# Changing the order of the high and low matmuls in a few groups of a one-core diffusion backbone

## The chip, the core and the metric

The kernel runs on one core of a Trainium2 chip. The metric is the device time of one execution in microseconds. Three executions of the kernel before were timed, and one more was run under the hardware profiler; the trace of that one is what all rows below come from.

## The reference, cut to what matters

The model has two layers over 256 latent tokens of width 2048, with a context prefix of 256 tokens. What bears on the change is the large projections: tall fp32 products of 256 tokens with weight matrices that are each used once.

```
# layer 0 (retention and Fourier mixing, gated)
yx = concat(retention(q, k, v) * silu(ga), fourier(u) * silu(gb)) @ w_out      # 4096 -> 2048
x  = x + gate_x * yx
# layer 1 (short gated convolution)
bg, cg, xt, g = split(h @ w_in, 4)                                             # 2048 -> 4 x 4096
y  = bg * conv3(cg * xt) * silu(g)
x  = x + gate_x * (y @ w_out)                                                  # 4096 -> 2048
return rmsnorm(x, final_norm_w)
```

## The kernel before

All activations are kept transposed, channels on partitions and 256 tokens along the free dimension. To keep fp32 accuracy with TensorE's fp32r format, every operand is split into a high part and a low part that is the rest. An activation tile holds both beside each other, high in columns 0 to 255 and low in columns 256 to 511. A weight tile of 1 MB (`raw`, 128 partitions by 2048) comes by DMA and is cut in four quarters of 512 columns: ScalarE casts a quarter into `whi` (line 94), VectorE subtracts and writes `wlo` (line 59). Each of the two has six buffers.

`group_t` (line 131) computes 256 output channels for 256 tokens into one PSUM tile `gT` with two halves of 128 channels, m = 0 and 1. It goes over `nkt` weight tiles (4 in the two output projections, 2 elsewhere), each with four quarters. A quarter holds four 128 by 128 blocks, j = 0 to 3, for two slices of input channels and the two halves m = j mod 2. Each block takes two matmuls: the **high** one, H, with the block of `whi` against all 512 columns of the activation (high and low part), and the **low** one, L, with the block of `wlo` against the 256 high columns. A pair H and L is so 768 columns. In the rows a high matmul reads `gT<-...,whi` with 128x512, and a low one `gT<-...,wlo` with 128x256. Each matmul has its own weight load (`LDWEIGHTS`, engine PEld).

The order of the eight matmuls of a quarter is one of three lists, written out by hand:

```
LOW = "L0 H0 L1 H1 L2 H2 L3 H3".split()
HIGH = "H0 L0 H1 L1 H2 L2 H3 L3".split()
MIRRORED = "H0 L0 L1 H1 H2 L2 L3 H3".split()
```

`LOW` is the rule. With `settle` set, the first weight tile of the group has its quarters in the order LOW, MIRRORED, MIRRORED, HIGH, and the rest of the group is LOW again. This is set in nine groups: in `project` (line 816), which runs for the output projection of layer 0 (`w0o`) and of layer 1 (`w1o`), for output blocks 1 and 3 of 8; and in the loop of layer 1 over 16 channel blocks (line 874), where each block has four groups in a row (`tcg`, `txt`, `tbg`, `tg`), in `tcg` of blocks 1, 2 and 8 and in `tbg` of blocks 0 and 1. The last block of each projection uses `group_d` (line 156) instead, in which all matmuls are 256 columns wide, and the value projections of layer 0 use `group_n`, in which all are 512 wide.

A scheduler orders the instructions of an engine from the order of the code and an estimate of when operands are ready. Around the output projection of layer 0 it mixes groups with the Fourier work (`pz`, `pP`, `py`), and around block 0 of layer 1 it mixes two groups. From block 1 of layer 1 to the end of block 6 of `w1o` the groups stand one behind another on TensorE.

Of the kernel before, what the change touches and what calls it, by code (L numbers as in the profile page):

```python
# [35 lines left out]
def body(tc, a, out):  # L36
    nc = tc.nc
    es = ExitStack()
    with es:
# [6 lines left out]
        def psum(name):  # L46
            return pp.tile([P, 2, 512], F32, tag="ps", name=name)

        def bank(name):
            return ap.tile([P, 512], F32, tag="bk", name=name)  # L50

        def act_tile(tag, name):
            return acts.tile([P, 2, 512], F32R, tag=tag, name=name)

        def mm(o, l, r, start, stop):
            nc.tensor.matmul(o, l, r, start=start, stop=stop, skip_group_check=True)  # L56
# [4 lines left out]
        def mul(o, x, y):  # L61
            nc.vector.tensor_tensor(o, x, y, op=ALU.mult)

        def add(o, x, y):
            nc.vector.tensor_tensor(o, x, y, op=ALU.add)  # L65
# [17 lines left out]
        def load_raw(src):  # L83
            raw = wp.tile([P, 2048], F32, tag="raw", name="raw")
            nc.sync.dma_start(raw[:], src)
            return raw
# [10 lines left out]
        def split_w(raw, spare=None):  # L97

            parts = []
            for pc in range(4):  # L100
                w = tuple(t[:] for t in spare()) if spare and pc == 3 else slot()
                cut(raw[:, pc * 512:(pc + 1) * 512], *w)
                parts.append(w)
            return parts
# [7 lines left out]
        def bg():  # L112

            if quiet[0]:
                return
            turn[0] ^= 1
            if tasks and (turn[0] or often[0]):
                tasks.pop(0)()

        def hook():  # L120
            if stages:
                f = stages.pop(0)
                if f is not None:
                    f()


        LOW = "L0 H0 L1 H1 L2 H2 L3 H3".split()
        HIGH = "H0 L0 H1 L1 H2 L2 H3 L3".split()
        MIRRORED = "H0 L0 L1 H1 H2 L2 L3 H3".split()

        def group_t(wd, i0, nkt, streams, settle=False):

            ps = [psum("gT") for _ in streams]
            last = nkt * 8 - 1
            for kt in range(nkt):
                raw = load_raw(wd[i0 + kt])
                bg()
                for pc, (hi, lo) in enumerate(split_w(raw)):
                    todo = LOW
                    if settle and kt == 0 and pc:  # L140
                        todo = HIGH if pc == 3 else MIRRORED
                    seen = set()
                    for what, j in ((x[0], int(x[1])) for x in todo):
                        k2, m = j // 2, j % 2
                        kc, c0 = kt * 8 + pc * 2 + k2, j * 128
                        n = 512 if what == "H" else 256
                        w = (hi if what == "H" else lo)[:, c0:c0 + 128]
                        for t, st in zip(ps, streams):
                            mm(t[:, m, 0:n], w, st[kc // 2][:, kc % 2, 0:n], kc == 0 and j not in seen,
                               kc == last and j in seen)  # L150
                        seen.add(j)
                    if pc % 2:
                        hook()
            return ps
# [40 lines left out]
        def lr(pool, t, name="t2", bufs=5, ring=5):  # L195

            r = pool.tile([P, 2, 256], F32, tag="t2", bufs=ring, name="lr_r")
            nc.scalar.copy(r[:], t[:, :, 256:512])  # L198
            s = pool.tile([P, 2, 256], F32, tag=name, bufs=bufs, name=name)
            add(s[:], t[:, :, 0:256], r[:])  # L200
            return s

        def rstd_bc(pool, ps_sum, n):

            r = pool.tile([P, 256], F32, tag="rstd", bufs=2, name="rstd")
            nc.scalar.activation(r[:], ps_sum, AF.Sqrt, bias=eps[:], scale=1.0 / n)
            nc.vector.reciprocal(r[:], r[:])
            return r
# [277 lines left out]
        for pr in range(4):  # L486
# [23 lines left out]
            def heads():  # L510
                return [retention(hh, mk[hh], q, k, kc, lambda: vbox[0]) for hh in range(2)]

            if pr == 0:
# [4 lines left out]
                h0, h1 = heads()  # L518
                stages += [None, h0[0], h1[0], h0[1], h0[2], h1[1], None, h1[2]]
                keep((pvx, pvc))  # L520
            elif pr < 3:
                k, kc = keys()
                q = queries()
                h0, h1 = heads()
# [3 lines left out]
            else:  # L528
# [6 lines left out]
                h0, h1 = heads()  # L535
# [8 lines left out]
            for hh, hd in enumerate((h0, h1)):  # L544
                y = yA[2 * pr + hh] = act_tile(YA[2 * pr + hh], f"yA{2 * pr + hh}")
                t = hd[3]["t"]
# [269 lines left out]
        def project(wd, xs, gcol, xin, acc, first=None, post=None):  # L816


            def res(b, m, v, src):
                nc.vector.scalar_tensor_tensor(x1[b][:, m, :], v, mods[:, gcol + 2 * b + m:gcol + 2 * b + m + 1],  # L820
                                               src[:, m, :], op0=ALU.mult, op1=ALU.add)

            tot = None
            for b in range(8):
                src = xin(b)
                quiet[0] = b >= 7 - (post is not None)
                if b < 7:
                    t = first if b == 0 and first is not None else group_t(wd, 4 * b, 4, [xs], b in (1, 3))[0]
                    s = lr(l1, t)
                    for m in range(2):  # L830
                        res(b, m, s[:, m, :], src)
                    if b == 0:
                        nc.scalar.square(acc[:], x1[b][:])
                    else:
                        sq = l1.tile([P, 2, 256], F32, tag="t2", bufs=5, name="sq")
                        nc.scalar.square(sq[:], x1[b][:])
                        add(acc[:], acc[:], sq[:])
                    for m in range(2 if post is not None else 0):
                        nc.scalar.activation(x1[b][:, m, :], x1[b][:, m, :], AF.Copy,
                                             scale=cols[:, post + 2 * b + m:post + 2 * b + m + 1])  # L840
                else:
                    t = group_d(wd, 4 * b, 4, xs)
                    tot = bank("tot")
                    for m in range(2):
                        mm(tot[:, 0:256], ones[:], acc[:, m, :], m == 0, False)

                    warm = l1.tile([P, 1], F32, tag="warm", name="warm")
                    nc.scalar.activation(warm[:], acc[:, 0, 0:1], AF.Sqrt)
                    sq = l1.tile([P, 2, 256], F32, tag="t2", bufs=5, name="sq")
                    for m in range(2):  # L850
                        res(b, m, t[:, m * 256:m * 256 + 256], src)
                        nc.scalar.square(sq[:, m, :], x1[b][:, m, :])
                        mm(tot[:, 0:256], ones[:], sq[:, m, :], False, m == 1)
            return rstd_bc(l1, tot[:, 0:256], D)
# [13 lines left out]
        h1 = [act_tile(HF[e], f"h1_{e}") for e in range(8)]  # L868
# [3 lines left out]
        w1 = a["w1"]  # L872
        y1 = []
        for b in range(16):
            settle = b in (1, 2, 8)
            tcg, = group_t(w1, b * 8, 2, [h1], settle)
            scg = lr(l1, tcg, "scg", 2)
            txt, = group_t(w1, b * 8 + 2, 2, [h1])
            z = lr(l1, txt, "z", 2)
            mul(z[:], z[:], scg[:])  # L880
            cv = l1.tile([P, 2, 256], F32, tag="cv", bufs=2, name="cv")
            for m in range(2):
                w = [cols[:, C_CV + j * 32 + 2 * b + m:C_CV + j * 32 + 2 * b + m + 1] for j in range(3)]
                z4 = z[:, m, :].rearrange("p (r w) -> p r w", w=64)
                c4 = cv[:, m, :].rearrange("p (r w) -> p r w", w=64)
                nc.vector.tensor_scalar(cv[:, m, :], z[:, m, :], w[1], None, op0=ALU.mult)
                nc.vector.scalar_tensor_tensor(c4[:, :, 1:64], z4[:, :, 0:63], w[0], c4[:, :, 1:64],
                                               op0=ALU.mult, op1=ALU.add)
                nc.vector.scalar_tensor_tensor(c4[:, :, 0:63], z4[:, :, 1:64], w[2], c4[:, :, 0:63],
                                               op0=ALU.mult, op1=ALU.add)  # L890
            tbg, = group_t(w1, b * 8 + 4, 2, [h1], b < 2)
            sbg = lr(l1, tbg)
            mul(cv[:], cv[:], sbg[:])
            tg, = group_t(w1, b * 8 + 6, 2, [h1])
            sg = silu_lr(l1, tg, "t2", 5)
            mul(cv[:], cv[:], sg[:])
            y1.append(act_tile(YA[b] if b < 8 else f"hx{b - 8}", f"y1_{b}"))
            split_act(y1[b], cv[:])
            quiet[0] = False
# [123 lines left out]
```

## Time and profile before

| | before |
|---|---|
| median of three timed runs | 1832.64 us (1829.4 to 1835.16) |
| profiled execution: time | 1831.67 us |
| profiled execution: span from first to last instruction | 1829.8 us |
| TensorE busy (matmuls) | 1781.8 us, 97% of the span |
| VectorE busy, ScalarE busy | 68%, 49% |
| mean granted clock of TensorE | 0.991 |
| HBM traffic over the span | 218 GB/s |

Between the profiled execution's time and its span lie 1.87 us before the first and after the last instruction. A matmul's row gives its start exactly, but its duration overlaps the next one, so paces are read from starts or from counts over a stretch, not from durations.

### The profile page before, as it was taken

How to read it: one execution, taken by the hardware profiler on the slowest of the kernel's cores; microseconds unless marked ns; L12 is line 12 of the kernel's file. 1: busy time of each engine (PE TensorE's matmuls, PEld its weight loads, DVE VectorE, ACT ScalarE, POOL GpSimd, SP SyncE). 2: the span in 40 equal slices, each digit the busy share in tenths (PEclk: the TensorE clock that was granted, in tenths of full speed). 3: DMA queues.
4: the chain of work that ended last, by engine and by line, in shares of the span. 5: the costliest groups of instructions: out<-in, count | busy, mean ns of one | idle time of the engine just before them, and what ended most of it. 6: DMA issues, size and time to landing. Idle time of an engine off the chain costs nothing.

```text
span 1829.8 us, 25929 instructions
## 1 busy us (share of the span) xinstructions
PE 1781.8 (97%) x10086; PEld 1514.5 (83%) x10086; DVE 1248.8 (68%) x2001; ACT 902.6 (49%) x1493; POOL 0.2 (0%) x4
## 2 busy tenths in 40 slices
PE   5999999999999999999999999999999999999997
PEld 3667888888877888888888888888888888888887
DVE  5348857768469788777688887666666666665554
ACT  4225626345455555445455555555455455455553
POOL 0000000000000000000000000000000000000000
PEclk9999999999999999999999999999999999999999
DMA  9886656665435555687548777555555555555552
GB/s 393 329 317 268 230 207 230 231 218 207 171 119 209 204 188 203 227 303 290 213 148 297 285 287 267 189 184 188 189 189 189 189 185 184 184 184 188 189 189 102
DMA packets 58732, 400.82 MB, mean 219 GB/s; under 512 B 6512, under 2 KB 6896, under 8 KB 11376
## 3 DMA queue, kind: packets, MB, share of 16 engines
q1 hardware_dynamic: 58608, 399.16, 59.7%
q8 instruction: 79, 1.29, 0.3%
q14 instruction: 45, 0.37, 0.1%
HBM read 397.03 MB, written 2.10 MB: 218 GB/s over the span
## 4 chain that ended last, share of the span: by engine, by line
PE 94%; DVE 3%; DMA 1%; issue 1%; ACT 1%; SPq 0%; DVEq 0%
PE gT L56 71%; PE gN L56 7%; PE gD L56 3%; PE pu L56 2%; PE gemv L56 2%; PE o L56 2%; PE pvx L56 1%; PE pk L56 1%; PE pvc L56 1%; DMA raw<-adaT 1%; PE pd L56 1%; PE S L56 1%; DVE wlo L59 1%; PE pq L56 1%; PE pP L56 1%
## 5 line engine op out<-in xcount | busy, mean ns | idle before, releaser
L94 ACT CAST whi<-raw 128x512 fp32r<-128x512 f32 x1024 | 629.0, 620 | 639.4 <-PE gT L56 465.8
L59 DVE TENSOR_TENSOR wlo<-raw,whi 128x512 fp32r<-128x512 f32 x1024 | 695.0, 689 | 358.5 <-ACT whi L94 351.2
L56 PE MATMUL gT<-h,whi 128*128 128x512 f32 x2048 | 718.4, 398 | 0.1
L56 PE MATMUL gT<-h,wlo 128*128 128x256 f32 x2048 | 568.5, 280 | 3.4 <-ACT h L214 3.4
L56 PEld LDWEIGHTS gT<-h,whi 128*128 128x128 f32 x2048 | 383.9, 188 | 91.2 <-DVE h L215 0.4
L56 PEld LDWEIGHTS gT<-h,wlo 128*128 128x128 f32 x2048 | 387.3, 189 | 6.5 <-ACT h L214 3.8
L56 PE MATMUL gT<-hx,whi 128*128 128x512 f32 x576 | 208.4, 397 | 0.0
L388 DVE CUSTOM_DVE_ANT_0 raw<-raw,scb 128x2048 f32<-128x2048 f32 x64 | 146.6, 2291 | 54.0 <-DMA raw<-adaT 50.7
L56 PE MATMUL gT<-hx,wlo 128*128 128x256 f32 x576 | 164.6, 286 | 2.7 <-ACT v L507 1.6
L56 PE MATMUL gT<-y,whi 128*128 128x512 f32 x448 | 156.8, 397 | 0.0
L56 PEld LDWEIGHTS gT<-hx,whi 128*128 128x128 f32 x576 | 108.5, 188 | 21.4
L56 PE MATMUL gT<-y,wlo 128*128 128x256 f32 x448 | 123.7, 280 | 0.0
L56 PEld LDWEIGHTS gT<-hx,wlo 128*128 128x128 f32 x576 | 109.1, 189 | 9.4 <-ACT v L507 2.1
L56 PEld LDWEIGHTS gT<-y,whi 128*128 128x128 f32 x448 | 83.5, 188 | 19.7
L198 ACT COPY lr_r<-gT 128x512 f32<-128x512 f32 x103 | 60.3, 585 | 69.1 <-PE gT L56 68.8
L56 PEld LDWEIGHTS gT<-y,wlo 128*128 128x128 f32 x448 | 84.5, 189 | 0.9
L56 PE MATMUL gT<-yA,whi 128*128 128x512 f32 x224 | 78.7, 395 | 0.0
L56 PE MATMUL gT<-yB,whi 128*128 128x512 f32 x224 | 78.5, 395 | 0.0
L65 DVE TENSOR_TENSOR t<-gT,lr_r 128x512 f32<-128x512 f32 x68 | 46.9, 690 | 31.1 <-ACT lr_r L198 31.0
L56 PE MATMUL gT<-yB,wlo 128*128 128x256 f32 x224 | 62.2, 278 | 0.0
L56 PE MATMUL gT<-yA,wlo 128*128 128x256 f32 x224 | 60.9, 279 | 0.6 <-DVE wlo L59 0.6
L94 ACT CAST whi<-ef 128x512 fp32r<-128x512 f32 x64 | 39.0, 620 | 42.4 <-DVE ef L65 19.4
(283 smaller groups left out, 2178.1 us busy)
## 6 DMA issues: line engine op xcount, KB each, us to landing
raw<-w SPq DMA_DIRECT2D x168, 1024.0 KB, 4.8
raw<-adaT SPq DMA_DIRECT2D x64, 1024.0 KB, 5.1
raw<-ada SPq DMA_DIRECT2D x32, 1024.0 KB, 7.8
raw<-w0o SPq DMA_DIRECT2D x32, 1024.0 KB, 4.9
raw<-w1o SPq DMA_DIRECT2D x32, 1024.0 KB, 4.8
raw<-w0g SPq DMA_DIRECT2D x16, 1024.0 KB, 4.8
raw<-w0u SPq DMA_DIRECT2D x16, 1024.0 KB, 4.8
raw<-w0s SPq DMA_DIRECT2D x8, 1024.0 KB, 7.3
```

The lines of the kernel that those rows point to most:

```text
L56: nc.tensor.matmul(o, l, r, start=start, stop=stop, skip_group_check=True)
L59: nc.vector.tensor_tensor(o, x, hi.bitcast(F32), op=ALU.subtract)
L65: nc.vector.tensor_tensor(o, x, y, op=ALU.add)
L94: nc.scalar.copy(hi, x)
L198: nc.scalar.copy(r[:], t[:, :, 256:512])
L388: nc.vector.tensor_tensor_reduce(out=raw[:], in0=raw[:], in1=scb[:], scale=1.0, scalar=0.0, op0=ALU.mult, op1=ALU.add, accum_out=gv[:, j:j ...
```

## The change

The mirrored quarters go. A new order, `FOURS`, has the four high matmuls of a quarter and then its four low ones. The argument `settle` is replaced by a pair of orders: the first is for the very first quarter of a group, the second for all its other quarters. `SETTLE` is HIGH and then FOURS for the whole rest of the group; `AFTER` is HIGH once and then LOW. A group with SETTLE is always followed by one with AFTER, in four places: blocks 1 and 2 of each output projection, and `tcg` and `txt` of blocks 1 and 2 of layer 1. All other groups are LOW throughout. The number of matmuls and weight loads, their shapes and their sums are as before.

```
-        MIRRORED = "H0 L0 L1 H1 H2 L2 L3 H3".split()
-
-        def group_t(wd, i0, nkt, streams, settle=False):
+        FOURS = "H0 H1 H2 H3 L0 L1 L2 L3".split()
+
+        SETTLE, AFTER = (HIGH, FOURS), (HIGH, LOW)
+
+        def group_t(wd, i0, nkt, streams, orders=(LOW, LOW)):
...
-                    todo = LOW
-                    if settle and kt == 0 and pc:
-                        todo = HIGH if pc == 3 else MIRRORED
+                    todo = orders[kt + pc > 0]
...
-                    t = first if b == 0 and first is not None else group_t(wd, 4 * b, 4, [xs], b in (1, 3))[0]
+                    t = first if b == 0 and first is not None else group_t(wd, 4 * b, 4, [xs], *({1: (SETTLE,), 2: (AFTER,)}.get(b, ())))[0]
...
-            settle = b in (1, 2, 8)
-            tcg, = group_t(w1, b * 8, 2, [h1], settle)
+            tcg, = group_t(w1, b * 8, 2, [h1], *((SETTLE,) if b in (1, 2) else ()))
...
-            txt, = group_t(w1, b * 8 + 2, 2, [h1])
+            txt, = group_t(w1, b * 8 + 2, 2, [h1], *((AFTER,) if b in (1, 2) else ()))
...
-            tbg, = group_t(w1, b * 8 + 4, 2, [h1], b < 2)
+            tbg, = group_t(w1, b * 8 + 4, 2, [h1])
```

First place, TensorE, `tcg` of block 1 of layer 1 (PSUM tile `gT_8757`), at the step from its first quarter (activation `h1_0`) to its second (`h1_1`). Before:

```order
L56 MATMUL gT_8757<-h1_0_8250,wlo_8764 128x256
L56 MATMUL gT_8757<-h1_0_8250,whi_8763 128x512
L56 MATMUL gT_8757<-h1_1_8251,whi_8767 128x512
L56 MATMUL gT_8757<-h1_1_8251,wlo_8768 128x256 x2
L56 MATMUL gT_8757<-h1_1_8251,whi_8767 128x512 x2
L56 MATMUL gT_8757<-h1_1_8251,wlo_8768 128x256 x2
L56 MATMUL gT_8757<-h1_1_8251,whi_8767 128x512
L56 MATMUL gT_8757<-h1_2_8252,whi_8771 128x512
```

The same place with the change:

```order
L56 MATMUL gT_8757<-h1_0_8250,whi_8763 128x512
L56 MATMUL gT_8757<-h1_0_8250,wlo_8764 128x256
L56 MATMUL gT_8757<-h1_1_8251,whi_8767 128x512 x4
L56 MATMUL gT_8757<-h1_1_8251,wlo_8768 128x256 x4
L56 MATMUL gT_8757<-h1_2_8252,whi_8771 128x512 x4
L56 MATMUL gT_8757<-h1_2_8252,wlo_8772 128x256 x4
```

Runs of two equal matmuls have become runs of four, and they go on to the end of the group, seven quarters in all.

Second place, TensorE, the step from `tcg` to `txt` of the same block (`gT_8757` to `gT_8865`). Before:

```order
L56 MATMUL gT_8757<-h1_7_8257,wlo_8826 128x256
L56 MATMUL gT_8757<-h1_7_8257,whi_8825 128x512
L56 MATMUL gT_8865<-h1_0_8250,wlo_8872 128x256
L56 MATMUL gT_8865<-h1_0_8250,whi_8871 128x512
L56 MATMUL gT_8865<-h1_0_8250,wlo_8872 128x256
```

With the change:

```order
L56 MATMUL gT_8757<-h1_7_8257,whi_8825 128x512 x4
L56 MATMUL gT_8757<-h1_7_8257,wlo_8826 128x256 x4
L56 MATMUL gT_8865<-h1_0_8250,whi_8871 128x512
L56 MATMUL gT_8865<-h1_0_8250,wlo_8872 128x256
L56 MATMUL gT_8865<-h1_0_8250,whi_8871 128x512
L56 MATMUL gT_8865<-h1_0_8250,wlo_8872 128x256
L56 MATMUL gT_8865<-h1_0_8250,whi_8871 128x512
L56 MATMUL gT_8865<-h1_0_8250,wlo_8872 128x256
L56 MATMUL gT_8865<-h1_0_8250,whi_8871 128x512
L56 MATMUL gT_8865<-h1_0_8250,wlo_8872 128x256
L56 MATMUL gT_8865<-h1_1_8251,wlo_8876 128x256
L56 MATMUL gT_8865<-h1_1_8251,whi_8875 128x512
```

Four pairs with the high matmul first now follow the last run of four low ones, and where LOW takes over again two low matmuls stand next to each other. The same sequence stands behind each of the four SETTLE groups.

Third place, TensorE, `tcg` of block 8 of layer 1 (`gT_11850`), its second quarter. Before:

```order
L56 MATMUL gT_11850<-h1_0_8250,wlo_11854 128x256
L56 MATMUL gT_11850<-h1_0_8250,whi_11853 128x512
L56 MATMUL gT_11850<-h1_1_8251,whi_11857 128x512
L56 MATMUL gT_11850<-h1_1_8251,wlo_11858 128x256 x2
L56 MATMUL gT_11850<-h1_1_8251,whi_11857 128x512 x2
L56 MATMUL gT_11850<-h1_1_8251,wlo_11858 128x256 x2
```

With the change:

```order
L56 MATMUL gT_11850<-h1_0_8250,wlo_11854 128x256
L56 MATMUL gT_11850<-h1_0_8250,whi_11853 128x512
L56 MATMUL gT_11850<-h1_1_8251,wlo_11858 128x256
L56 MATMUL gT_11850<-h1_1_8251,whi_11857 128x512
L56 MATMUL gT_11850<-h1_1_8251,wlo_11858 128x256
L56 MATMUL gT_11850<-h1_1_8251,whi_11857 128x512
```

Low and high now alternate through the whole of block 8, and so from `txt` of block 2 to block 0 of the last projection without a break. On VectorE and SyncE the scheduler shifts a few instructions by a place or two around the SETTLE groups; one such shift in the first projection puts a 128x2048 reduction (line 388) ahead of the split of an activation tile (`yB`, line 59) instead of behind it.

## Rows read from the trace of the kernel before

**Rows 1.** The page: busy time of each engine, and the chain that ended last.

```profile
PE 1781.8 (97%) x10086; PEld 1514.5 (83%) x10086; DVE 1248.8 (68%) x2001; ACT 902.6 (49%) x1493; POOL 0.2 (0%) x4
...
PE 94%; DVE 3%; DMA 1%; issue 1%; ACT 1%; SPq 0%; DVEq 0%
```

**Rows 2.** What TensorE waited for: us in total, times, longest us.

```profile
PE gT L56 <- DVE wlo L59: 1.7, 3, 0.8
```

**Rows 3.** All waits from 760 us on: us in total, times, longest us.

```profile
ACT whi L94 <- PE gT L56: 403.0, 583, 1.5
```

**Rows 4.** gT's instructions by stretch: length, busy (xcount) by engine, clock, DMA.

```profile
777.00:797.00 20.00, 20.00 (x115) 17.33 (x114) 0.00 (x0) 0.00 (x0) 1.00 0.80 304
803.00:886.00 83.00, 83.00 (x481) 72.56 (x480) 2.08 (x3) 1.75 (x3) 1.00 0.78 288
946.00:966.00 20.00, 20.00 (x116) 17.39 (x115) 1.38 (x2) 1.17 (x2) 1.00 0.63 226
969.00:987.00 18.00, 18.00 (x106) 15.78 (x105) 1.19 (x2) 1.18 (x2) 1.00 0.82 289
991.00:1009.00 18.00, 18.00 (x104) 15.60 (x103) 0.69 (x1) 1.17 (x2) 1.00 0.80 305
1014.00:1275.00 261.00, 261.00 (x1508) 228.25 (x1508) 15.92 (x23) 13.74 (x24) 1.00 0.64 234
1280.00:1660.00 380.00, 380.00 (x2153) 329.45 (x2152) 22.45 (x33) 19.35 (x33) 1.00 0.53 187
1665.00:1705.00 40.00, 40.00 (x233) 34.95 (x232) 1.39 (x2) 1.17 (x2) 1.00 0.55 195
1709.00:1793.00 84.00, 84.00 (x478) 72.80 (x477) 2.07 (x3) 1.76 (x3) 1.00 0.52 187
```

**Rows 5.** TensorE's timeline, tcg of layer 1's block 2: start us, us, instruction.

```profile
1009.39 0.63 PE L56 MATMUL gT<-h,whi 128*128 128x512 f32 x2
1009.86 0.39 PE L56 MATMUL gT<-h,wlo 128*128 128x256 f32 x2
1010.09 0.63 PE L56 MATMUL gT<-h,whi 128*128 128x512 f32 x2
...
1012.17 0.63 PE L56 MATMUL gT<-h,whi 128*128 128x512 f32 x2
...
1013.45 0.40 PE L56 MATMUL gT<-h,whi 128*128 128x512 f32 x1
1013.69 0.40 PE L56 MATMUL gT<-h,wlo 128*128 128x256 f32 x2
```

**Rows 6.** The same at the end of block 8's mirrored quarters.

```profile
1279.75 0.40 PE L56 MATMUL gT<-h,whi 128*128 128x512 f32 x1
1279.98 0.40 PE L56 MATMUL gT<-h,wlo 128*128 128x256 f32 x2
```

**Rows 7.** gN's instructions (all 512 columns) in one stretch, columns as above.

```profile
437.00:477.00 40.00, 40.00 (x178) 33.10 (x178) 0.09 (x1) 1.00 0.48 174
```

**Rows 8.** gD's instructions (all 256 columns) in one stretch.

```profile
888.00:908.00 20.00, 20.00 (x169) 20.00 (x168) 0.00 (x0) 1.00 0.56 203
```

**Rows 9.** TensorE's timeline: low matmuls of two alternating stretches, each entered from Fourier work.

```profile
654.25 0.28 PE L56 MATMUL gT<-hf,wlo 128*128 128x256 f32 x1
...
656.38 0.28 PE L56 MATMUL gT<-hf,wlo 128*128 128x256 f32 x1
...
690.93 0.28 PE L56 MATMUL gT<-hf,wlo 128*128 128x256 f32 x1
...
692.66 0.28 PE L56 MATMUL gT<-hf,wlo 128*128 128x256 f32 x1
```

**Rows 10.** Timeline, first projection: the shifted split and reduction, and the split's use.

```profile
751.19 0.69 DVE L59 TENSOR_TENSOR yB<-yf,yB 128x512 fp32r<-128x512 f32 x1 [0.69 <-ACT yB L220]
751.80 2.29 DVE L388 CUSTOM_DVE_ANT_0 raw<-raw,scb 128x2048 f32<-128x2048 f32 x1
...
755.15 0.28 PE L56 MATMUL gT<-yB,wlo 128*128 128x256 f32 x1
```

## The prediction

> **What bounds the kernel now.** I read the page first. TensorE's matmuls are busy for 97% of the span and the chain that ended last runs on TensorE for 94% of it [rows 1]. Then the waits. TensorE waited for low parts of weights three times in the whole execution, 1.7 us together [rows 2]. The other way round, from 760 us on, ScalarE's casts waited 403.0 us for TensorE to give back a weight buffer [rows 3]. So the weights are ready before they are needed, and the time is TensorE's own pace. Nothing that VectorE, ScalarE or the DMA queues do is late enough to matter in the stretches that the change touches; the clock is granted in full in all of them [rows 4].
>
> The pace is the next thing to look at, and it has to be looked at by stretches. Count gT's matmuls in a stretch, take one away for the one that hangs over the edge, and halve the count for pairs of one high and one low matmul. From 1014 to 1275 us that is 753.5 pairs in 261.00 us, 346.4 ns each. From 1280 to 1660 us it is 1076 pairs in 380.00 us, 353.2 ns each [rows 4]. These are the same matmuls in the same alternating order on the same activations, with the clock at 1.00 in both. TensorE has two steady paces for one and the same instruction stream, 6.8 ns a pair apart (2%), and it keeps the one it is in for hundreds of microseconds. The seven shorter stretches are of one kind or the other, alternately: 777 slow (20.00 us for 57 pairs, 351), 803 fast (346), 946 slow (348, with too few pairs to tell by itself), 969 fast (343), 991 slow (350), 1665 fast (345), 1709 slow (352). The short ones are uncertain by one matmul, some 3 ns.
>
> What lies between the nine stretches is the point. Each of the eight boundaries but the one from 886 to 946 us, where other work runs, is a group with mirrored quarters, seven in all, and each of the seven changes the pace: slow to fast near 800, 967, 1011 and 1662 us, fast to slow near 989, 1277 and 1707 us. The mirrored quarters act like a switch that toggles. The one in block 8, near 1277 us, threw a fast engine back into the slow pace for the longest stretch of the kernel.
>
> **The change, part by part.** *Mirrored quarters removed.* They cost nothing in themselves: eight pairs between 1009.39 and 1012.17 us take 2.78 us, 347.5 ns each [rows 5]. What goes is the toggling. Block 8 gets none, so whatever pace holds after block 2 of layer 1 now holds to block 0 of the last projection.
>
> *Runs of four.* 7 quarters in each of two groups of layer 1 and 15 in each of two projection groups are 44 quarters, 176 pairs. The trace of before has no run of four high and four low. From below, streams of one width alone: 512 wide 40.00 us for 177, 226.0 ns [rows 7]; 256 wide 20.00 us for 168, 119.0 ns [rows 8]; the sum, 345, is 1.4 ns under the fast pace, a gain of 0.2 us at most. From above, I take the slow pace, as the worst steady pace seen: 176 x 6.8 ns = 1.2 us. The alternation of widths is what costs in both paces and there is less of it here, but some is left, so I take +0.6 us, near the middle.
>
> *The high part first in eight groups.* A high matmul needs only the cast, so it can start before the subtraction is done. It can win at most the 1.7 us [rows 2] and most of that lies elsewhere: 0. A buffer of high parts also comes free after the fourth matmul of a quarter instead of near the eighth, which helps ScalarE, and ScalarE only waits for TensorE anyway [rows 3]: 0.
>
> *Shifted instructions.* In the first projection a reduction of 2.29 us goes ahead of the split of `yB`. The split started at 751.19 us and would start some 2.3 us later, ending near 754.2 us; its first use is at 755.15 us [rows 10]. Hidden, with about 0.9 us to spare. Without that cover it would cost up to 1.4 us.
>
> *The pace after the four places.* This decides. Behind each SETTLE group the same sequence stands: a run of four low matmuls, four pairs with the high one first, then two low ones together and alternation. The long regular run before it should wipe out what pace the engine came with, so that all four places leave it in the same pace. If it is the fast one, the slow stretches behind the places become fast: 777 to 797 us 57 pairs, 991 to 1009 us 51.5, 1280 to 1660 us 1076, 1709 to 1793 us 238.5 [rows 4], together 1423 pairs x 6.8 ns = 9.7 us. The stretch from 946 us lies ahead of the first place in layer 1 and stays.
>
> Sum, against the profiled execution's own time: 1831.67 - 9.7 + 0.6 = 1822.6 us. That execution lies 0.97 us below the median of the timed runs, inside their spread, so I give 1823 us as the forecast.
>
> **Why the fast pace.** The evidence is thin here, and I choose by it. In all seven places where the pace changed, the last thing before the new steady pace was this change-over: four pairs with the high one first, then two low matmuls together. In block 2 the double low came 0.24 us after the high one at 1013.45 and the fast pace followed [rows 5]; in block 8 it came 0.23 us after the high one at 1279.75 and the slow pace followed [rows 6]. So it matters at which point of the engine's rhythm the double comes, and a fixed sequence ahead of it fixes that point. Which point it will be, the trace cannot say: an alternation that begins behind a long run of low matmuls is slow from 654.25 us (6 pairs in 2.13 us, 355 ns) and fast from 690.93 us (5 pairs in 1.73 us, 346 ns) [rows 9]. Against that even count stands that slow engines left the mirrored quarters fast four times of four, and that an engine behind a run of fours comes with a disturbed rhythm, more like those than like the steady fast one.
>
> **The rivals.** *All four places end in the slow pace* (the other side). Then the stretches that are fast now lose: 803 to 886 us 240 pairs, the part of 969 to 987 us that is `txt`, 32 pairs, 1014 to 1275 us 753.5 pairs, and 1665 to 1705 us without the SETTLE group's own 48 pairs, 68 [rows 4]. That is 1093.5 x 6.8 ns = 7.4 us: 1831.67 + 7.4 + 0.6 = 1839.7 us, slower by 0.4%. For it speaks the entry at 654.25 us, against it the four of four. It is decided at the double low matmul behind the second SETTLE group of layer 1, near 1018 us, since 1829.5 of the pairs follow from there.
>
> *The places end differently.* If layer 1 stays slow from its second place on and the projections are fast, 1831.67 - 0.4 (777 to 797 us) + 0.2 (`txt`) + 5.1 (1014 to 1275 us) - 1.6 (1709 to 1793 us) + 0.6 = 1835.6 us, 0.2% slower. If layer 1 alone is fast and the projections slow, 1831.67 - 7.7 + 1.6 + 0.5 + 0.6 = 1826.7 us, 0.3% faster. Against both: the same sequence stands at all four places. For them: a wait inside a place can shift the rhythm, and the run of fours in the first projection is broken up by other work.
>
> *The order does not set the pace.* Then the two paces have another cause, such as the DMA traffic beside them, and the toggling at seven of seven places is chance. Only the runs of four would count: 1831.7 to 1832.3 us. DMA shares speak against it: the fast long stretch has 0.64 and the slow one, with less traffic, 0.53 [rows 4]. The Trainium skill, TensorE: Matmul & The Clock Gate, section Back-to-back issue gap, takes this side: it gives a matmul's gap by its width alone, and by its isolated formula a pair of 512 and 256 columns would be an estimated 325 ns in any order, which would make the whole change worth nothing. This trace disagrees, with 346.4 and 353.2 ns for one order, so the rows decide.
>
> **How the numbers follow.** Chances: all places fast 0.58, all slow 0.22, places that differ 0.14 (0.08 for a slow layer 1, 0.06 for a fast one), no effect of the order 0.06. About 0.3%, 5.5 us, is what a measurement of this kernel can tell from no change. The first case is faster, the second slower; of the mixed ones and of no effect nearly all lie within. That makes faster 0.60, same 0.17, slower 0.23. The first case by itself goes from 1820 (runs of four at the fast pace, and a timed run as far below its fellows as the fastest of before) to 1826 us. The range has to take in the mixed cases as well and leaves out the slow one: 1819 to 1837 us.
>
> **What would show it.** Pairs at 346 to 347 ns from `txt` of layer 1's block 2 to the last projection's block 0, some 640 us without a change, show the main term right; 353 ns there shows it wrong. The first projection from its block 2 and the last from its block 2 should have the pace of layer 1. In a SETTLE group eight pairs should take between 2.76 and 2.83 us. If the pace changes where no order changes, or differs behind equal places, the idea of a fixed exit is wrong. A wait for low parts near 755 us would put the shifted reduction on the path.

## The result, and the profile after

| | before | after |
|---|---|---|
| median of four timed runs | 1831.99 us (1829.40 to 1835.16) | 1840.76 us (1839.72 to 1842.94) |
| ratio, with 95% interval | | 1.005 (1.0036 to 1.0064) |
| profiled execution: time, span | 1831.67, 1829.8 us | 1841.37, 1839.6 us |

The kernel became 0.5% slower where 0.5% faster was forecast. The time lies 1.1 us from the rival of the prediction that went to the other side, all four places in the slow pace, 1839.7 us.

The page of after, its lines on busy time and on the chain that ended last, looks as before [rows 1].

```profile
PE 1792.6 (97%) x10086; PEld 1520.6 (83%) x10086; DVE 1247.6 (68%) x2001; ACT 901.6 (49%) x1493; POOL 0.2 (0%) x4
...
PE 94%; DVE 2%; DMA 2%; ACT 1%; issue 0%; SPq 0%; DVEq 0%; ACTq 0%
```

TensorE is the bound with the same share, and it is busy 10.8 us longer with the same number of matmuls. Two answers on waits: what TensorE waited for in the whole execution, and ScalarE's longest from 760 us on (us in total, times, longest us).

```profile
PE gT L56 <- DVE wlo L59: 1.2, 1, 1.2
```

```profile
ACT whi L94 <- PE gT L56: 397.4, 562, 1.5
```

They answer to [rows 2, 3]. TensorE has no new wait that is long enough to explain the loss: it is pace again. (The one wait of 1.2 us lies at 583 us, ahead of the change, where before waited 0.8.) gT's instructions by stretch, in the columns of [rows 4]:

```profile
779.00:890.00 111.00, 111.00 (x631) 96.29 (x630) 3.33 (x5) 2.35 (x4) 1.00 0.77 286
941.00:965.00 24.00, 24.00 (x137) 20.81 (x137) 2.07 (x3) 1.76 (x3) 1.00 0.50 175
981.00:1012.00 31.00, 31.00 (x177) 26.89 (x177) 1.42 (x3) 1.17 (x2) 1.00 0.81 296
1025.00:1667.00 642.00, 642.00 (x3636) 556.74 (x3635) 38.21 (x56) 32.28 (x55) 1.00 0.57 202
1692.00:1803.00 111.00, 111.00 (x630) 96.22 (x630) 2.84 (x5) 2.35 (x4) 1.00 0.52 183
```

Counted as in the prediction, the long stretch has 1817.5 pairs at 353.2 ns, and the others 352 to 353. All five stretches are slow. Before, 1094 of these pairs ran at 346.4 [rows 4].

Where the time went can be followed by numbering TensorE's matmuls from 0 to the last and taking the start of the same number in both traces. This is after minus before, in us:

```
matmul number                2800   3200   3800   4000   4800   5600   7200   8800   last
its start before             554    634    735    766    899    1042   1320   1603   1819
after minus before           +0.4   +3.7   +3.7   +2.9   +4.4   +4.6   +9.1   +9.1   +9.8
```

It grows where before was fast (4.5 us between numbers 5600 and 7200, which is most of 1014 to 1275 us), and it stands still where before was slow too. The 9.8 us have three parts: 3.7 up to number 3800, a gain of 0.8 at number 3840, and 6.8 behind it (3.72 - 0.78 + 6.83 = 9.77). Number 3840 is the first matmul that the change touches, at the start of the first SETTLE group. TensorE's timeline there, before and after:

```profile
740.05 0.28 PE L56 MATMUL pz<-wlo,ch 128*128 128x256 f32 x1
740.94 0.39 PE L56 MATMUL gT<-yA,wlo 128*128 128x256 f32 x1 [0.62 <-DVE wlo L59]
```

```profile
743.77 0.28 PE L56 MATMUL pz<-wlo,ch 128*128 128x256 f32 x1
743.89 0.40 PE L56 MATMUL gT<-yA,whi 128*128 128x512 f32 x1
```

Before, the group began with a low matmul and TensorE waited for its low part; in after a high one goes first and waits for nothing, so 0.89 us from start to start became 0.12. Of the kernels below, the two that begin this group with a low matmul (e4, e9) have 0.76 and 0.80 us there, and the other ten 0.12. The change's own part is so 9.77 - 3.72 = 6.05 us, some 6.1.

The 3.7 us ahead of it are not its doing: 3.3 of them come up between numbers 2800 and 3200, in code that is the same in both kernels. One row of all instructions for that stretch (length, busy and count of TensorE, its weight loads, VectorE, ScalarE, GpSimd, clock, DMA), first of after, then of before:

```profile
615.00:655.00 40.00, 40.00 (x213) 33.70 (x212) 26.99 (x48) 16.51 (x32) 0.00 (x0) 0.87 0.46 158
```

```profile
615.00:655.00 40.00, 40.00 (x233) 33.45 (x232) 29.79 (x53) 19.02 (x36) 0.00 (x0) 0.96 0.48 169
```

TensorE was never idle in either, but its granted clock was 0.87 and 0.96, so it was at the lower level, 1.2 GHz, for longer in after, and 20 fewer matmuls got through. That varies between executions, as two kernels below that are the same up to 700 us show: 0.91 and 0.83 from 615 to 635 us. What TensorE did before is much the same, too: it was busy 18.6 us of the 20 from 575 to 595 us in after, 19.2 in before, and without a gap from 595 us in both.

### The profile page after: what moved, and what is told of

Read it like the earlier page. It is cut to its first block, busy times and chain, and to the rows that moved or that the text cites. A ratio compares the mean times of both kernels' runs of the same rounds, so it can differ in the third digit from the quotient of the medians.

```text
span 1839.6 us, 25958 instructions
## 1 busy us (share of the span) xinstructions
PE 1792.6 (97%) x10086; PEld 1520.6 (83%) x10086; DVE 1247.6 (68%) x2001; ACT 901.6 (49%) x1493; POOL 0.2 (0%) x4
## 4 chain that ended last, share of the span: by engine, by line
PE 94%; DVE 2%; DMA 2%; ACT 1%; issue 0%; SPq 0%; DVEq 0%; ACTq 0%
PE gT L56 71%; PE gN L56 7%; PE gD L56 2%; PE pu L56 2%; PE gemv L56 2%; PE o L56 2%; PE pk L56 1%; PE pvc L56 1%; PE pvx L56 1%; DMA raw<-ada 1%; PE S L56 1%; PE pd L56 1%; DMA raw<-w0s 1%; PE pP L56 1%; DVE wlo L59 1%; PE pz L56 1%
## 5 line engine op out<-in xcount | busy, mean ns | idle before, releaser
L59 DVE TENSOR_TENSOR wlo<-raw,whi 128x512 fp32r<-128x512 f32 x1024 | 693.1, 688 | 352.1 <-ACT whi L94 346.4
L56 PE MATMUL gT<-y,wlo 128*128 128x256 f32 x448 | 118.4, 281 | 0.0
L56 PE MATMUL gN<-whi,hx 128*128 128x512 f32 x192 | 59.7, 392 | 0.0
```

The lines of the kernel that those rows point to most:

```text
L59: nc.vector.tensor_tensor(o, x, hi.bitcast(F32), op=ALU.subtract)
```

## The experiments

**The theories.** Theory A: alternation has two steady paces, and which of them follows is decided by the point of the engine's rhythm at which two equal matmuls stand next to each other. The rivals: the runs of four themselves lead to the slow pace, whatever stands behind them; or chance picks the pace in each execution.

The rhythm can be read from the starts of the matmuls. These are the gaps in ns from each matmul's start to the next, from the traces, in pairs (high's gap, low's gap):

```
slow pace, after    233 117 | 241 120 | 236 113 | 233 117 | 241 120 | 236 113 | ...   sum of three pairs 1060 = 3 x 353.3
fast pace           231 112 | 233 117 | 231 113 | 232 118 | ...                       346.7 a pair
```

The slow pace repeats every three pairs. Here is TensorE's timeline of after at the first exit in layer 1, from the last runs of four of `tcg` to `txt` of block 1 (start us, us, instruction).

```profile
975.57 1.09 PE L56 MATMUL gT<-h,whi 128*128 128x512 f32 x4
976.50 0.63 PE L56 MATMUL gT<-h,wlo 128*128 128x256 f32 x4
976.97 1.09 PE L56 MATMUL gT<-h,whi 128*128 128x512 f32 x4
977.89 0.64 PE L56 MATMUL gT<-h,wlo 128*128 128x256 f32 x4
978.37 0.40 PE L56 MATMUL gT<-h,whi 128*128 128x512 f32 x1
978.61 0.28 PE L56 MATMUL gT<-h,wlo 128*128 128x256 f32 x1
978.72 0.40 PE L56 MATMUL gT<-h,whi 128*128 128x512 f32 x1
978.96 0.28 PE L56 MATMUL gT<-h,wlo 128*128 128x256 f32 x1
979.08 0.40 PE L56 MATMUL gT<-h,whi 128*128 128x512 f32 x1
...
979.43 0.40 PE L56 MATMUL gT<-h,whi 128*128 128x512 f32 x1
979.67 0.40 PE L56 MATMUL gT<-h,wlo 128*128 128x256 f32 x2
979.90 0.40 PE L56 MATMUL gT<-h,whi 128*128 128x512 f32 x1
```

The two quarters of four from 975.57 to 978.37 take 2.80 us for eight pairs. The four pairs with the high one first then already go at the slow rhythm: 0.35, 0.36, 0.35 us from high to high. The double low at 979.67 falls behind the fourth of them, whose high gap is 233, and nothing changes. Theory A says that the same double two pairs earlier, or four later, would fall behind a pair with 241 and set the engine free.

**e1_exit8, e2_exit2, e3_exit3: only the length of the high-first part is changed.** After has four pairs before the double low. These have eight, two and three. The index of the order counts quarters in all of them.

```
-        SETTLE, AFTER = (HIGH, FOURS), (HIGH, LOW)
+        SETTLE, AFTER = (HIGH, FOURS), (HIGH, HIGH, LOW)       # e1
+        EXIT = "H0 L0 H1 L1 L2 H2 L3 H3".split()               # e2
+        EXIT = "H0 L0 H1 L1 H2 L2 L3 H3".split()               # e3
+        SETTLE, AFTER = (HIGH, FOURS), (EXIT, LOW)             # e2, e3
...
-                    todo = orders[kt + pc > 0]
+                    todo = orders[min(4 * kt + pc, len(orders) - 1)]
```

> The changed kernel with one thing altered: behind each SETTLE group eight pairs with the high matmul first instead of four, so the double low matmul comes four pairs later. Theory A (the place of the double low in TensorE's three-pair rhythm decides the pace): in the changed kernel the pairs behind the run of fours go 234/117, 241/120, 236/113, 233/117 ns, and the double after the fourth left the slow pace. After the eighth it falls behind the pair 241/120, the place at which the mirrored quarters of before went from slow to fast. So 346.7 ns a pair behind all four places; 315 + 91 + 1819 + 315 pairs gain 6.7 ns each, 17 us: 1823 to 1825 us. Theory B (a run of fours leaves the slow pace whatever follows): no change, 353.3 ns and 1840 to 1842 us. Theory C (only mirrored quarters, low pairs next to high pairs, make the fast pace): also 1840 to 1842 us.

> The changed kernel with the double low matmul two pairs behind the run of fours instead of four. Theory A: the double falls behind the second pair, 241/120 ns, so the pace is fast (346.7 ns) behind all four places and the time 1823 to 1825 us. Theories B and C: slow, 1840 to 1842 us.

> The changed kernel with the double low matmul three pairs behind the run of fours. Theory A: the double falls behind the third pair, 236/113 ns, the place at which block 8's mirrored quarters of before stayed slow (double low 0.23 us after its high matmul): 353.3 ns a pair, 1840 to 1842 us. Theory B: the same. A theory D, that any exit shorter or longer than four pairs is fast, says 1823 to 1825 us.

Measured: e1 1824.40 us (1823.35 to 1825.79, four runs) beside 1833.73 of before on the same chip, ratio 0.9944 (0.9927 to 0.9961). e2 1823.42 and e3 1826.41 us, one run each. gT by stretch, e1:

```profile
782.00:890.00 108.00, 108.00 (x626) 94.45 (x624) 2.77 (x4) 2.35 (x4) 1.00 0.78 286
981.00:1010.00 29.00, 29.00 (x169) 25.35 (x168) 1.38 (x2) 1.18 (x2) 1.00 0.80 294
1025.00:1654.00 629.00, 629.00 (x3632) 550.09 (x3631) 38.04 (x55) 32.28 (x55) 1.00 0.58 206
1680.00:1787.00 107.00, 107.00 (x620) 93.54 (x619) 2.77 (x4) 2.35 (x4) 1.00 0.53 187
```

The long stretch has 346.5 ns a pair, and all four places end fast. The turn is visible at the first exit in layer 1, where the double low comes at 980.33, behind the eighth pair:

```profile
980.09 0.40 PE L56 MATMUL gT<-h,whi 128*128 128x512 f32 x1
980.33 0.40 PE L56 MATMUL gT<-h,wlo 128*128 128x256 f32 x2
980.57 0.40 PE L56 MATMUL gT<-h,whi 128*128 128x512 f32 x1
```

So four more quarters with the high one first, with nothing else touched, turn a loss of 0.5% into a gain of 0.6%. The runs of four do not decide, and the rival that says so falls. e2 was fast behind all places too. Which of the places bear on theory A is seen below. e3 was half a miss:

```profile
778.00:889.00 111.00, 111.00 (x630) 96.31 (x629) 3.08 (x5) 2.35 (x4) 1.00 0.75 282
979.00:1011.00 32.00, 32.00 (x183) 27.75 (x183) 2.07 (x3) 1.18 (x2) 1.00 0.82 301
1024.00:1654.00 630.00, 630.00 (x3637) 550.96 (x3636) 38.52 (x56) 32.28 (x55) 1.00 0.58 207
1679.00:1788.00 109.00, 109.00 (x631) 95.32 (x630) 3.26 (x5) 2.35 (x4) 1.00 0.53 187
```

Its first two places end slow (353 and 352 ns), as theory A had it, but the last two end fast (346.5 and 346.0), behind the very same exit. What differs is the run of four before it. The gaps of its last quarter and of what follows:

```
                       last quarter of four               | high first              | double low and on
after, block 1         235 234 236 224 117 120 120 120    | 234 117 241 120 236 113 233 | 117 121 237 118 236 116 224 117 234 117 241  slow
e2, block 1            235 234 235 225 117 120 120 120    | 233 118 241             | 120 120 236 120 230 113 232 118 231         fast
e3, block 1            235 233 236 224 117 120 120 120    | 234 117 241 120 236     | 113 119 234 117 241 120 236 113 233         slow
e3, block 2            233 236 229 232 118 119 117 117    | 235 117 230 116 230     | 117 118 233 117 231 113 232 118 230         fast
```

There are two kinds of quarter of four. In a run they take turns. Call X the kind whose last two low gaps are 116 to 118, and Y the one whose last three are about 120. Behind Y the alternation starts in the slow rhythm; behind X it is fast at once, and a double low does not undo that here. A run with an odd number of quarters (seven or 15) ends with the kind that it began with, so that the phase with which the engine came survives the run. Which kind comes first shows in the pairs ahead of the run: in all 14 whole runs of after, e1, e2, e3, e5 and e6 it is Y behind pairs of 230 and 117, where the engine was just set free, and X behind 241 120 236 113, the slow rhythm. In after, the three whole runs of seven and 15 quarters begin and end with Y: the doubled high matmul with which a SETTLE group starts fell behind a 241 each time and set the engine free, and the run with its exit gave the pace away again.

This also bounds what e1 and e2 show. Only in the first projection and in block 1 does their run end with Y, so only there is it the point of the double low that made them fast. In block 2 and in the last projection their engine came fast, the doubled high matmul ahead of the run made it slow, the run began and ended with X, and the fast pace of the long stretch follows from that.

**e5_seven and e6_six: the length of the run.** To test the two kinds alone, both keep only the places of the first projection and of block 1. In e6 the group of block 1 has six quarters of four instead of seven.

```
-        SETTLE, AFTER = (HIGH, FOURS), (HIGH, LOW)
+        SETTLE, AFTER = (HIGH, FOURS), (HIGH, LOW)
+        SIX = (HIGH, HIGH, FOURS)
...
-            tcg, = group_t(w1, b * 8, 2, [h1], *((SETTLE,) if b in (1, 2) else ()))
+            tcg, = group_t(w1, b * 8, 2, [h1], *((SETTLE,) if b == 1 else ()))      # e5
+            tcg, = group_t(w1, b * 8, 2, [h1], *((SIX,) if b == 1 else ()))         # e6
```

> The changed kernel with its SETTLE and AFTER groups only in the first projection and in block 1 of layer 1; block 2 of layer 1 and the last projection are LOW throughout. Twin of the next run. Theory A2: in a run of fours quarters of two kinds take turns, X (high 233 236 228 233, low 117 120 117 117 ns) and Y (235 233 236 224, 117 120 120 120); behind X the engine is fast at once, behind Y slow; an engine that enters at the fast pace, as all four places of the changed kernel did, starts with Y, and seven quarters end with Y. So slow, 353.3 ns a pair from block 1 to the end, 1840 to 1842 us. Theory B (a run of fours leaves the slow pace): the same.

> As the run before, but the group in block 1 has two quarters with the high matmul first and then six of fours instead of one and seven. Theory A2: it starts with Y as before and ends with X after six, so the engine leaves it fast and stays so through layer 1 and the last projection: some 2336 pairs at 346.7 instead of 353.3 ns, 15.6 us less than its twin, 1824.5 to 1827 us. Theory B, or that the run wipes out all that came before it and always ends alike: slow, 1840 to 1842 us.

Measured in one run each: 1839.83 and 1826.87 us. gT from block 1 to the end, e5 and then e6:

```profile
979.00:1801.00 822.00, 822.00 (x4654) 713.22 (x4653) 45.16 (x66) 38.16 (x65) 1.00 0.57 205
```

```profile
981.00:1788.00 807.00, 807.00 (x4658) 705.73 (x4658) 44.98 (x66) 38.29 (x65) 1.00 0.58 209
```

One stretch of over 800 us each, at 353.3 and 346.6 ns a pair. One quarter in another order, eight matmuls of 10086, moves the time by 13.0 us. By matmul numbers it is 15.2 us from number 4000 on, since e6 came there 2.1 us late; the 2328.5 pairs of e6's row give 2328.5 x 6.7 ns = 15.6.

**e4_alllow: no settling at all.** `SETTLE, AFTER = (LOW,), (LOW,)`.

> No settling anywhere: every group in the order LOW. All theories have the slow pace from the end of the first projection's Fourier work, as the changed kernel has it. Against the changed kernel only the runs of four go, whose 176 pairs took about 351 ns in its trace: with 353.3 ns that is 0.4 us more, 1840 to 1842 us. If it is faster than that, the four places of the change do harm rather than nothing; if the pace changes somewhere without any settling group, the pace is not set by order alone.

Measured: 1842.09 us (1839.54 to 1846.95, six runs), ratio 1.0045 (1.0029 to 1.0062). gT from layer 1's first groups to the last projection's end:

```profile
939.00:1800.00 861.00, 861.00 (x4875) 746.67 (x4874) 48.43 (x70) 40.75 (x70) 1.00 0.57 206
```

353.3 ns throughout: after is worth as much as no settling.

**e7_high1, e8_high2, e12_high3: one doubled matmul at three points.** No mirrored quarters and no runs of four in layer 1 and the last projection: LOW up to a certain group of block 1, HIGH from there to the end. At the change-over two high matmuls stand together, once. In e7 HIGH begins with the second group of block 1, in e8 with the third, in e12 with the fourth. For e7, and in the same way for the other groups:

```
-            txt, = group_t(w1, b * 8 + 2, 2, [h1], *((AFTER,) if b in (1, 2) else ()))
+            txt, = group_t(w1, b * 8 + 2, 2, [h1], (HIGH,) if 4 * b + 1 >= 5 else (LOW,))
```

> No run of fours and no double low matmul in layer 1 and the last projection: LOW up to the first group of block 1 and HIGH in every group from the second group of block 1 on, so that there is one place with two high matmuls together and nothing else. Theory A: what counts is only where in the slow rhythm of three pairs (high to low 241, 236, 233 ns) the doubled matmul falls. In the changed kernel two high matmuls together behind the 241 brought the fast pace at block 1's first group; this place lies 36 pairs later, at the same point of the rhythm. So fast from 977 us on, 2336 pairs, 1825 to 1827 us. Theory C (mirrored quarters needed) or E (the low part first is what is slow, or the reverse): see the next run, which E would have at the same pace as this one; C has both slow, 1841 to 1843 us.

> As the run before, with the switch from LOW to HIGH one group later, at the third group of block 1: 32 pairs later, two further on in the rhythm of three. Theory A: the doubled high matmul falls behind the 233, where the traces so far kept the slow pace: 353.3 ns to the end, 1841 to 1843 us, 15 to 16 us above its twin with one group fewer in the new order. Theory E (high first is the fast order by itself): fast, 1825 to 1827 us.

> The switch from LOW to HIGH at the fourth group of block 1, 64 pairs behind the fast one, the one point of the rhythm of three not tried so: the doubled high matmul falls behind the 236. Theory A: slow, as in the stretch of before's layer 1 in which such a double kept the slow pace; 1841 to 1843 us. Fast would mean that two of three points release the engine.

Measured in one run each: 1822.97, 1843.13 and 1840.79 us. gT before and behind the doubled matmul, e7 and e8:

```profile
938.00:974.00 36.00, 36.00 (x206) 31.23 (x205) 2.77 (x4) 2.35 (x4) 1.00 0.61 214
976.00:1784.00 808.00, 808.00 (x4664) 712.72 (x4663) 45.07 (x66) 37.59 (x66) 1.00 0.58 209
```

```profile
943.00:990.00 47.00, 47.00 (x268) 40.81 (x267) 3.45 (x5) 2.67 (x5) 1.00 0.65 228
992.00:1804.00 812.00, 812.00 (x4598) 704.23 (x4597) 44.38 (x65) 37.24 (x64) 1.00 0.57 204
```

e7 goes from 351 to 346.6 ns, e8 stays slow (352, then 353.3). e12 stayed at 353.3 to the end as well. Of the 20.2 us between e7 and e8, 16.1 come up from matmul number 4000 on. The gaps up to that of the first of the two high matmuls, and from the second one's on:

```
e7    232 118 240 120 236 114 232 118 240 | 238 116 231 116 230 117 230    fast
e8    232 118 241 120 236 113 233         | 236 115 225 117 233 118 241    slow
e12   236 113 233 117 241 120 236         | 227 113 233 117 241 120 236    slow
```

With block 1 of e1 and e2 (two lows, behind 241), of e3 (behind 236) and of after (behind 233), all three points of the slow rhythm have been tried with two lows and with two highs: behind 241 the engine is set free, behind the other two it is not. The seven mirrored groups of before agree: the double low that ended them came behind 241 in the four that left fast, and behind 235 or 236 in the three that left slow.

**e11_high1_again, e10_best: is it chance, and what is the best?** e11 is e7 again, timed. e10 adds the exit of e2 in the first projection.

> The same kernel as the run that switches once to HIGH at the second group of block 1, now timed. If the pace is fixed by the order alone and not by chance, every execution has the fast pace: all within 1822 to 1828 us. If the pace were drawn anew in each execution, single times would come near 1842 us.

> LOW up to block 1 of layer 1 and HIGH from its second group to the end, as in the run that was fast, and in the first projection SETTLE with the double low matmul two pairs behind the run of fours. Theory A: fast from the first projection's block 2 (315 pairs more than in the run without that, 2.1 us) and from 975 us to the end: 1820 to 1824 us by the median, 0.6% below before and 1.1% below the changed kernel.

Measured: e11 1823.64 us (1822.35 to 1827.09, five runs), ratio 0.9953 (0.9940 to 0.9966). e10 1823.77 us (1822.60 to 1825.92, five runs), ratio 0.9952 (0.9939 to 0.9965). Five runs within 5 us, where the paces are 15 us apart, so the order of the instructions picks the pace in each execution and not chance. e10's first projection was fast (109 us for 315 pairs from 778 us, 346.0 ns), but the 2.1 us that this saves do not show in the median. By matmul numbers they are there, between 4000 and 4800; the spans of the profiled executions, 1821.9 and 1820.8 us, differ by 1.1 us only, since e10 lost 1.7 us against e11 between numbers 2800 and 3200, where after lost its 3.3. All instructions from 615 to 635 us, e11 and then e10, with the clock at 0.91 and 0.83:

```profile
615.00:635.00 20.00, 20.00 (x117) 16.68 (x117) 13.01 (x24) 7.25 (x15) 0.00 (x0) 0.91 0.47 172
```

```profile
615.00:635.00 20.00, 20.00 (x107) 16.82 (x106) 11.76 (x23) 6.80 (x14) 0.00 (x0) 0.83 0.43 165
```

**e9_before_no8: the kernel before without its one bad place.** `settle = b in (1, 2)` instead of `b in (1, 2, 8)`; `tbg` of blocks 0 and 1 keeps its mirrored quarters.

> The kernel before with one thing taken away: no settling in block 8 of layer 1, its other eight settling groups as they were. Theory A: the mirrored quarters toggle. Without block 8's the fast pace goes on from 1014 us to the end of layer 1 (1076 pairs gain 6.7 ns, 7.2 us); block 1 of the last projection then throws it into the slow pace (116 pairs lose 0.8 us) and block 3 brings it back (239 pairs gain 1.6 us): 8 us less than before. Theory F (block 8's settling helps, and the pace would have fallen back there anyhow): no change or slower.

Measured: 1824.36 us (1823.41 to 1825.24, four runs), ratio 0.9955 (0.9939 to 0.9971).

```profile
1015.00:1275.00 260.00, 260.00 (x1502) 227.29 (x1501) 15.90 (x23) 13.59 (x24) 1.00 0.64 234
1280.00:1652.00 372.00, 372.00 (x2148) 325.19 (x2147) 22.13 (x32) 18.85 (x32) 1.00 0.54 190
1658.00:1698.00 40.00, 40.00 (x229) 34.67 (x228) 0.79 (x2) 1.17 (x2) 1.00 0.54 189
1704.00:1785.00 81.00, 81.00 (x470) 70.80 (x469) 2.07 (x3) 1.77 (x3) 1.00 0.53 189
```

The fast pace of block 2 now holds through block 8 (346.5 ns from 1280 us on), the same double in the last projection's block 1 then makes a fast engine slow (351), and the next one makes it fast again (345). This one line of the kernel before gives as much as the best new order that was tried (1823.64 us, e11).

## Why the prediction was wrong

**The bound, and the two paces: right.** TensorE's pace is all that moved, 6.7 ns a pair between the two as measured over the long stretches of e5 and e6.

**Runs of four, +0.6 us: right.** In after two quarters took 1400 + 1406 ns by starts (2.80 us for eight pairs in the rows above), 350.8 ns a pair: 176 x (350.8 - 346.7) = 0.7 us against the fast pace.

**High part first: put at 0, and it gained 0.8 us.** The prediction set it to nothing because most of the 1.7 us of waits for low parts lies elsewhere. One of the three waits, 0.62 us at 740.94 us, lay at the start of the first SETTLE group, and it is gone in after. The freer buffers of high parts: right at nothing, as TensorE did not wait for a cast in the stretches of the change.

**The shifted reduction: right.** The reduction, the split and the split's first use in after:

```profile
754.22 2.29 DVE L388 CUSTOM_DVE_ANT_0 raw<-raw,scb 128x2048 f32<-128x2048 f32 x1 [0.88 <-DMA raw<-adaT]
...
756.44 0.69 DVE L59 TENSOR_TENSOR yB<-yf,yB 128x512 fp32r<-128x512 f32 x1
...
758.08 0.28 PE L56 MATMUL gT<-yB,wlo 128*128 128x256 f32 x1
```

The split ends at 757.13 and is used 0.95 us later; 0.9 us to spare were forecast.

**The pace after the four places: wrong, and this alone made the forecast wrong.** The prediction said: "The long regular run before it should wipe out what pace the engine came with, so that all four places leave it in the same pace. If it is the fast one, the slow stretches behind the places become fast." The places did agree, but in the slow pace: in place of -9.7 us came +6.1, the 6.8 us behind number 3840 less the 0.7 of the runs of four. Two steps under it failed. First, a run of fours does not wipe out the rhythm that the engine came with: its quarters take turns between two kinds, and seven or 15 of them hand on the phase (e3's block 2 against its block 1, e6 against e5). Second, the count of four slow engines that left the mirrored quarters fast was taken as evidence for this exit. In all four of those places the double low came behind a pair with a gap of 241, as the gaps of the kernel before show: near 1013.5 us 224 117 234 117 241 and then the double, and near 1279.8 us, where the engine was thrown into the slow pace, 241 120 236 and then the double. The gaps stood in the trace from the start and would have shown a rhythm of three. The prediction came as far as "it matters at which point of the engine's rhythm the double comes", and stopped at the sums over whole stretches.

**The rival that came true** had 7.4 + 0.6 = 8.0 us. The medians differ by 8.8 us; the traces by 9.8, of which 3.7 lie ahead of the change and 6.1 are its own. That the median came within 1.1 us of this rival's time is so in part luck. "Against it the four of four" was the wrong weight, for the reason above. The rival that the order does not set the pace is refuted by e5 and e6. The Trainium skill, TensorE: Matmul & The Clock Gate, section Back-to-back issue gap, gives a formula for the gap at the full clock in which the matmul's width alone counts. Here the same widths in the same order have 346.6 or 353.3 ns a pair for 800 us, so the measurement decides against it for such a stream.

**What stays open.** What it is in TensorE that has a rhythm of three pairs, and why a double behind 241 ends it, no run here shows: the phase is described, not explained. Nor is it shown why the granted clock falls for longer near 615 us in some executions, which moves a time by some 3 us.

## What to carry to other kernels

Where TensorE is the bound with 97%, count its matmuls by stretch: equal work at unequal pace with a full clock was worth 15.6 us here, where the waits for weights that the change touched were worth 0.8. Then read the gaps from start to start, not only their mean, and look for the period. If a pace keeps itself, find the right point of the period for the one irregular step in the trace, put it there once and leave it, as e7 does with a single change-over, rather than repeat it: each repetition (block 8 of before) can throw the engine back.

## What was not expected of the hardware

- An alternation of matmuls 512 and 256 columns wide has two paces that keep themselves, 346.6 and 353.3 ns a pair, for over 800 us each at a clock of 1.00, with equal DMA shares beside them (0.58 and 0.57).
- The slow one has a period of three pairs (high gaps 241, 236, 233 ns). One doubled matmul, high or low, ends it behind the pair with 241 and not behind the other two.
- Four high and four low matmuls in turn have two kinds of quarter (1.401 and 1.406 us by starts) that alternate. The last one decides the rhythm in which the alternation behind it starts. Eight matmuls in another order moved the whole kernel by 13.0 us (e6 against e5, one run each).
- The same instructions ran at a granted clock of 0.96 or 0.87 from 615 to 655 us in different executions, worth 3.3 us.
